# Placing the operands of a matmul-bound hybrid block at a fixed distance in SBUF

## The chip, the cores and the metric

One NeuronCore of a Trainium2 chip runs the whole block. The metric is device time in microseconds of one execution, the median of several runs. Beside it there is one profiled execution of the same program, whose trace the views below read.

## The reference

One residual layer with two branches over 16 meta tokens and 512 tokens, model width 2048, all in float32:

```python
h = rms_norm(x, norm_g)
proj = h @ w_in                      # 2048 x 12368
(q_a, k_a, v_a, z_a, q_i, k_i, w_i, q_b, f_b, i_b, z_b, gates) = jnp.split(proj, cuts, axis=-1)
...
# branch A: per query a ReLU indexer scores the keys, the top 128 are kept, attention over them
o_a = dsa_attention(q, k, v, qi, ki, wi, chunk_ids, topk)
y_a = o_a.reshape(B, T, BRANCH_WIDTH) * jax.nn.silu(z_a)
# branch B: gated linear recurrence S_t = diag(f_t) S_{t-1} + k_t v_t^T, chunkwise
o_b = rms_norm(hgrn2_chunkwise(qb, 1.0 - f, vb, jnp.log(f)), hgrn_out_norm_g)
y_b = o_b.reshape(B, T, BRANCH_WIDTH) * jax.nn.silu(z_b)
p = jnp.einsum('btnc,ncd->btnd', jnp.stack([y_a, y_b], axis=2), w_branch)
merged = jnp.sum(jax.nn.sigmoid(gates.reshape(B, T, N_BRANCH, D)) * p, axis=2)
return x + merged @ w_out
```

## The kernel before, in words

Every large product is made of three matmuls in the type float32r: an operand is split into a high part (the value rounded to float32r) and a low part (the rest), and high x high, high x low and low x high are summed in PSUM. ScalarE makes the high part of a weight, VectorE (or a DMA that adds) the low part; both are in the helper `hi_lo`, into the tiles `wh` and `wl`, which rotate over three buffers each.

The kernel walks through a list of jobs. The first are ordinary ("in"): the indexer's key and queries and two gates of branch B, with moving operands of 512 columns. Then come 43 pairs ("pair"): each takes two blocks of 128 columns of `w_in` and uses a Strassen-like scheme, in which seven products of half size take the place of eight. Tokens are split in two halves of 264 (8 meta tokens and 256 others), the 2048 rows of the weights in two halves of 1024. The seven products have names:

```python
SEVEN = (("11", "11", "x", 0), ("s2", "t2", "y", 0), ("12", "21", "x", 1), ("s3", "t3", "y", 1),
         ("s1", "t1", "z", 0), ("22", "t4", "w", 0), ("s4", "22", "z", 1))
```

The first column names the weight operand (a raw block or a sum of blocks), the second the token operand, the third the PSUM bank. Each product is 8 steps k of three matmuls, 24 in all, 168 in a pair. In pairs the weights are stationary and the tokens move, with 256 columns, or 264 where the meta tokens are wanted (`w=264`: key/value pairs and forget/input pairs). The token operands lie in `hH`, `hL` (16 tiles each, the two halves side by side, 1056 bytes apart) and in `tT` (the sums t1 and t2 in tiles `a` and `b`, t4 with its high part in the first half of a tile and its low part in the second). They are made once and stay to the end of the pairs.

After the pairs come 32 branch jobs ("br", 24 matmuls of 512 columns each; weights stationary, `yH` and `yL` moving), among which the attention of the eight heads is run, and at the end 8 output jobs ("out"), the same scheme as the pairs with the tokens (`mh`) stationary and the weights moving, 256 columns.

All temporaries and the long-lived token operands live in 70 equal slots of 528 float32 a partition, 2112 bytes, handed out by the class `Slots`. The program's order is written out by a planner: each engine has a clock, each instruction a cost, and a slot remembers when its last user ends by these clocks. `Slots.get` took the free slot that had been free longest. Work beside the matmuls (top-k, normalisation and rotation of queries and keys, the recurrence, the attention) is in tasks with priorities, which `pump` advances between the matmuls as long as the clocks of VectorE and ScalarE are not too far ahead of TensorE's. Each engine then runs its own instructions in that order. Weights arrive by SP's queue, sums of weight blocks are made by VectorE and by adding DMAs on POOL's queue, and a pair's results go to DRAM over SP's queue.

Beside the slots there are fixed tiles: `tabQ` and `tabK` (rotary tables multiplied by the norms' gains, made in `consts`), `MT`, and `bias0` to `bias3` for the top-k mask. `consts` was started at the eighth job, among the indexer's queries. Gate pairs (16 of them) are spread over the list by `gate_pair`.

A matmul's two operands are read at addresses in SBUF that follow from slot and weight tile. The slots begin 2112 bytes apart, which is 64 more than a multiple of 256. The weight tiles were 4096 bytes long and began at multiples of 256, and their parts are 512 or 1024 bytes long.

Of the kernel before, what the change touches and what calls it, by code (L numbers as in the profile page):

```python
# [38 lines left out]
SAME = {"pe": 0.0, "act": 60.0, "dve": 125.0, "pool": 60.0}  # L39
MARGIN = 300.0  # L40
NSLOT = 70
NZ = 2
# [103 lines left out]
class Slots:  # L146
    def __init__(self, core, pool, tags, shape, space):
        self.core, self.pool, self.shape = core, pool, shape
        self.free = list(tags)
        self.last = {t: (0.0, "pe") for t in tags}  # L150
        self.tag = {}
        self.k = 0
        self.peak = 0
        self.total = len(tags)

    def get(self, name, dt=F32):
        assert self.free, "out of " + name
        t = min(self.free, key=lambda x: self.last[x][0])
        self.free.remove(t)
        self.peak = max(self.peak, self.total - len(self.free))  # L160
        self.k += 1
        a = self.pool.tile(self.shape, dt, name=f"{name}_{self.k}", tag=t)
        nm = a.tensor.name
        self.tag[nm] = t
        self.core.ac[nm] = self.last[t]
        return a
# [17 lines left out]
def hybrid_kernel(ctx, tc, x, meta, vecs, w_in, rows, w_branch, w_out,  # L184
# [8 lines left out]
    E = Core(nc)  # L193
    S = Slots(E, sp, [f"s{i}" for i in range(NSLOT)], [128, T], None)
    B1 = Slots(E, pp, [f"b{i}" for i in range(6)], [128, 512], None)
    B2 = Slots(E, pp, ["c0"], [128, 2, 512], None)
# [67 lines left out]

    def slots(name, n=1, dt=F32):
        return [S.get(name, dt) for _ in range(n)]

    def slot(name, dt=F32):
        return S.get(name, dt)

# [20 lines left out]
    for c in range(2):  # L291
        s = wp.tile([128, 1024], F32, name=f"xm{c}", tag=f"wh{c}")
# [3 lines left out]
    tabs = slots("tabs", 2)  # L296
    tabA = tabs[0][:, 0:320].rearrange("p (b d) -> p b d", b=5)
    RB = tabs[0][:, 320:512]
    tabI = tabs[1][:, 0:160].rearrange("p (b d) -> p b d", b=5)
    wi = tabs[1][:, 160:224].rearrange("p (b d) -> p b d", b=4)  # L300
    masks = cp.tile([128, 256], U8, name="masks")
# [85 lines left out]

    def hi_lo(k, src, m):
        h = wp.tile([128, 1024], F32R, name=f"wh{k}", tag=f"wh{k % NWS}")
        l = wp.tile([128, 1024], F32R, name=f"wl{k}", tag=f"wl{k % NWS}")  # L390
        E.act(h[:, :m], src, AF.Copy)
        if 8 <= k < 22:
            n = l[:, :m]
            E.act(n, h[:, :m].bitcast(F32), AF.Copy, scale=-1.0)
            E.dma_add(n, src.bitcast(F32R))
        else:
            (E.ptt if k < 6 else E.tt)(l[:, :m], src, h[:, :m].bitcast(F32), OP.subtract)
        return h, l

    def split_chunk(k, ch):  # L400
        load_upto(ch["i"])
        m = ch["nk"] * ch["ncols"]
        r, nk, n = ch["raw"], ch["nk"], ch["ncols"]
        ch["h"], ch["l"] = [], []
        if k < 4:
            for g in range(2):
                h, l = slot("eh", F32R), slot("el", F32R)
                w = 4 * n
                E.act(h[:, :w], r[:, w * g:w * g + w], AF.Copy)
                (E.ptt if k > 1 else E.tt)(l[:, :w], r[:, w * g:w * g + w], h[:, :w].bitcast(F32), OP.subtract)  # L410
                early.extend((h, l))
                ch["h"] += [h[:, n * i:n * i + n] for i in range(4)]
                ch["l"] += [l[:, n * i:n * i + n] for i in range(4)]
        else:
            h, l = hi_lo(k, r[:, :m], m)
            ch["h"] = [h[:, n * i:n * i + n] for i in range(nk)]
            ch["l"] = [l[:, n * i:n * i + n] for i in range(nk)]
        load_upto(ch["i"] + NRAW)
# [22 lines left out]
    def prep_op(k, op):  # L441
# [20 lines left out]
    cvec = cp.tile([128, 35], F32, name="cvec")  # L462
    MT = cp.tile([128, 256], F32, name="MT")
    lbt = fp.tile([128, 8, 4], F32, name="lbt")
    gq1 = fp.tile([128, 2], F32, name="gq1")
    tabQ = cp.tile([128, 4, 64], F32, name="tabQ")
    tabK = cp.tile([128, 5, 64], F32, name="tabK")

    def consts():
# [11 lines left out]
        E.dve([gq1], [], 2, lambda v: v.memset(gq1[0:32, :], 1.0))  # L481
        for t, o, nb in ((tabQ, 64, 4), (tabK, 128, 5)):
# [86 lines left out]
    kk = []  # L569
    CQ, SQ = slot("cq"), slot("sq")  # L570

# [56 lines left out]
    def idx_task(j, xq):  # L628
# [53 lines left out]
        if not idx_left[0]:  # L682
            S.put(kkH, kkL, CQ, SQ, tabs[1])
            for qt in range(4):
                topk_tasks.append(spawn(topk_task(qt), 6))
# [6 lines left out]
    first_two = []  # L692
    bias = [cp.tile([128, k], BF16, name=f"bias{k}") for k in KQ]

# [89 lines left out]
    def tokens(src, x, d, tab, name):  # L784
# [23 lines left out]
        E.tt(yv, yv, r[:, None, 8:12, None].to_broadcast([128, 4, 4, 32]), OP.mult)  # L808
        yield E.clk["pe"]
        v = y[:, 0:128].rearrange("p (c d) -> p c d", c=4)  # L810
        a = sq[:, 0:128].rearrange("p (c d) -> p c d", c=4)
# [9 lines left out]
    def ka_task(g, xk):  # L821
        y = yield from tokens({(0, 256): xk[:, 8:264], (2, 256): xk[:, 272:528]}, xk, kd_[g][:, 16:528],
                              tabK[:, 0:4, :], "ka")
        yield from room(1)
# [3 lines left out]
        spawn(fan_out(kd_[g][:, 16:528], tb, e, ("k", g)), 0)  # L828
        if g == 3:
# [5 lines left out]
            y, e = yield from norm_rope(pb[:16].rearrange("p (b d) -> p b d", b=4), 16, 4,  # L835
                                        tabK[:16, 4:5, :].to_broadcast([16, 4, 64]), "km")
            B1.put(pb)
            yield e
            yield E.clk["pe"] + 3000.0
# [58 lines left out]
    def q_task(h, xq):  # L898
        y = yield from tokens({(0, 512): xq[:, :512]}, xq, qd_[h], tabQ, "qa")
# [4 lines left out]
        spawn(fan_out(qd_[h], tb, e, ("q", h)), 0)  # L904

    att, raws, got = {}, {}, set()
# [13 lines left out]
    def att_task(h):  # L920
# [22 lines left out]
        for qt in (3, 2, 1, 0):  # L943
# [6 lines left out]
            else:  # L950
                if qt:
                    pb = yield from bank("plg")
                vs[qt] = pb[:, :kq] if qt else pb[:, KQ[1]:KQ[1] + kq]
# [46 lines left out]
    def pv_task(h, ps, e):  # L1000
# [69 lines left out]
        yield e  # L1070
        yH[0, h], yL[0, h] = slot("yH", F32R), slot("yL", F32R)
        E.act(yH[0, h][:, :512], z[:, :512], AF.Copy)
# [18 lines left out]
    def hgrn_task(h, prev):  # L1091
# [6 lines left out]
        while not LB:  # L1098
            yield WAIT
        while ready() < 5:  # L1100
            yield WAIT
# [298 lines left out]
    def tops_task(i):  # L1400
# [3 lines left out]
        for k in range(4 * i, 4 * i + 4):  # L1404
# [320 lines left out]
    jobs[3].pre = pre_t  # L1725
    jobs[7].pre = lambda: spawn(consts(), 2)
    jobs[-1].pre = lambda: (sum_1(jobs[ji]), sum_2(jobs[ji]), hold.append(1))
# [16 lines left out]
    for h in range(0, 8, 2):  # L1744
        two(A[h], A[h + 1])
    for g in range(4):
# [4 lines left out]
        if g in (1,):  # L1751
            gate_pair()
    for h in range(8):
# [3 lines left out]
        if h == 0:  # L1757
            jobs[-1].pre = lambda: E.more.update(act=130.0, dve=85.0)
        for _ in range((1, 2, 1, 2, 1, 2, 1, 2)[h]):
            gate_pair()  # L1760
# [216 lines left out]
```

## Time and profile before

| | |
|---|---|
| median of 3 runs | 1481.22 us (1479.68 to 1481.84) |
| profiled execution | 1480.5 us, its span 1478.7 us |
| granted TensorE clock | 1.000 |
| TensorE busy | 1465.2 us, 12544 matmuls |
| VectorE busy | 1187.8 us |
| ScalarE busy | 712.6 us |
| GpSimd busy | 271.9 us |
| moved by DMA | 263.25 MB |

The span is the time from the first to the last instruction. Matmuls overlap in flight: one is recorded for about 0.28 us and the next starts well before it ends, so busy time says little about TensorE, and the distance from one start to the next is what is to be read. PE are the matmuls, PEld the loads of the stationary operand, DVE is VectorE, ACT ScalarE, POOL GpSimd. Addresses of operands are not in the profile; they are those of the compiled program.

### The profile page before, as it was taken

To read this page: it belongs to the slowest core of one execution; us is meant where nothing else is said; L and a number is where in the kernel's file an instruction comes from. 1 tells how busy PE (TensorE), PEld (TensorE's weight loads), DVE (VectorE), ACT (ScalarE), POOL (GpSimd) and SP (SyncE) were. 2 spreads that over 40 slices of the span, in tenths; PEclk is the share of its full clock that TensorE was granted. 3 is DMA by queue.
4 is the path that set the end of the run, shared out by engine and by line. 5 is a ranking of instruction groups with operands and counts; after the bars stand their busy time and mean duration, and the time that the engine had idled before them with its cause. 6 is when DMAs were issued, how large, how long until landed. Compare 5 with 4: busy or idle time off the path is not lost.

```text
span 1478.7 us, 31334 instructions
## 1 busy us (share of the span) xinstructions
PE 1465.2 (99%) x12544; PEld 1396.4 (94%) x12544; DVE 1187.8 (80%) x2017; ACT 712.6 (48%) x1170; POOL 271.9 (18%) x346
## 2 busy tenths in 40 slices
PE   7999999999999999999999999999999999999999
PEld 6888899999999999999999999999998888889998
DVE  6698899999998888788887887888676755878776
ACT  5576644444444454444444444444467752334332
POOL 2211000003313320101001011000367110103221
PEclk9999999999999999999999999999999999999999
DMA  9266577877888977767787686857896335448873
GB/s 275 76 158 152 143 172 186 188 182 193 214 210 218 240 173 183 179 168 182 172 194 165 171 193 158 200 144 191 198 286 167 111 109 155 147 131 221 213 212 90
DMA packets 336066, 263.25 MB, mean 178 GB/s; under 512 B 32484, under 2 KB 303408, under 8 KB 335920
## 3 DMA queue, kind: packets, MB, share of 16 engines
q1 hardware_dynamic: 306160, 174.51, 41.2%
q0 software_dynamic: 24256, 80.45, 28.1%
q10 hardware_dynamic: 5504, 6.29, 1.3%
q8 instruction: 98, 1.61, 0.4%
q14 instruction: 48, 0.39, 0.1%
HBM read 170.40 MB, written 29.98 MB: 136 GB/s over the span
## 4 chain that ended last, share of the span: by engine, by line
PE 97%; DVE 2%; ACT 0%; DMA 0%; issue 0%; POOL 0%; DVEq 0%; POOLq 0%
PE pg L93 20%; PE px L91 17%; PE pz L91 16%; PE py L91 16%; PE po L91 11%; PE pw L91 8%; PE psc L93 1%; PE phl L93 1%; PE pov L91 1%; PE plg L93 1%; PE pho L93 1%; PE ppt L97 1%; PE px L97 1%; PE phs L93 0%; DMA vrow<-in_vecs_dram 0%; PE pw L97 0%
## 5 line engine op out<-in xcount | busy, mean ns | idle before, releaser
L101 ACT ACTIVATE wh<-raw 128x1024 fp32r<-128x1024 f32 x305 | 323.4, 1061 | 483.5 <-PE pz L91 130.8
L108 DVE TENSOR_TENSOR wl<-raw,wh 128x1024 fp32r<-128x1024 f32 x289 | 356.6, 1234 | 100.5 <-ACT wh L101 99.5
L91 PE MATMUL px<-hH,wh 128*128 128x256 f32 (+1 forms) x688 | 195.6, 284 | 0.0
L91 PE MATMUL px<-hH,wl 128*128 128x256 f32 (+1 forms) x688 | 194.1, 282 | 0.0
L91 PE MATMUL px<-hL,wh 128*128 128x256 f32 (+1 forms) x688 | 193.6, 281 | 0.0
L101 ACT ACTIVATE wh<-sum 128x1024 fp32r<-128x1024 f32 x102 | 108.2, 1060 | 156.0 <-PE py L91 41.9
L91 PE MATMUL po<-wh,mh 128*128 128x256 f32 x896 | 158.0, 280 | 0.0
L108 DVE TENSOR_TENSOR wl<-sum,wh 128x1024 fp32r<-128x1024 f32 x102 | 131.0, 1284 | 29.2 <-ACT wh L101 28.6
L91 PEld LDWEIGHTS po<-wh,mh 128*128 128x128 f32 x896 | 137.1, 188 | 0.0
L91 PEld LDWEIGHTS px<-hH,wh 128*128 128x128 f32 x688 | 129.4, 188 | 0.5
L91 PEld LDWEIGHTS px<-hH,wl 128*128 128x128 f32 x688 | 129.5, 188 | 0.0
L91 PEld LDWEIGHTS px<-hL,wh 128*128 128x128 f32 x688 | 129.4, 188 | 0.0
L91 PE MATMUL pz<-tT,wh 128*128 128x256 f32 (+1 forms) x688 | 127.1, 284 | 0.0
L91 PE MATMUL pw<-tT,wh 128*128 128x256 f32 (+1 forms) x688 | 126.4, 284 | 0.0
L91 PE MATMUL po<-wl,mh 128*128 128x256 f32 x448 | 125.3, 280 | 0.0
L91 PE MATMUL py<-tT,wh 128*128 128x256 f32 (+1 forms) x688 | 125.2, 282 | 0.0
L117 POOL DMA_DIRECT2D raw<-raw x51 | 44.2, 868 | 363.2 <-DVE sum L108 340.6
L91 PEld LDWEIGHTS pz<-tT,wh 128*128 128x128 f32 x688 | 105.7, 188 | 0.2
L91 PEld LDWEIGHTS pw<-tT,wh 128*128 128x128 f32 x688 | 105.6, 189 | 0.2
L91 PEld LDWEIGHTS py<-tT,wh 128*128 128x128 f32 x688 | 105.7, 188 | 0.0
L93 PE MATMUL pg<-yH,wh 128*128 128x512 f32 x256 | 103.3, 403 | 0.0
L93 PE MATMUL pg<-yH,wl 128*128 128x512 f32 x256 | 101.0, 394 | 0.0
(319 smaller groups left out, 3870.8 us busy)
## 6 DMA issues: line engine op xcount, KB each, us to landing
raw<-in_w_in_dram SPq DMA_DIRECT2D x192, 512.0 KB, 4.6
raw<-raw POOLq DMA_DIRECT2D x51, 512.0 KB, 5.4
raw<-sum POOLq DMA_DIRECT2D x51, 512.0 KB, 5.4
raw<-in_w_branch_dram SPq DMA_DIRECT2D x32, 512.0 KB, 4.8
raw<-in_w_out_dram SPq DMA_DIRECT2D x32, 512.0 KB, 4.1
gd<-g SPq DMA_DIRECT2D x32, 256.0 KB, 4.5
g<-gd POOLq DMA_DIRECT2D x30, 256.0 KB, 3.3
wl<-raw POOLq DMA_DIRECT2D x14, 512.0 KB, 4.6
```

The costliest lines, as they stand in the source:

```text
L91: self.nc.tensor.matmul(out, lhsT, rhs, start=start, stop=stop, skip_group_check=True)
L93: self.nc.tensor.matmul(out, lhsT, rhs, start=start, stop=stop)
L97: self.nc.tensor.transpose(out, in_, ident)
L101: self.nc.scalar.activation(out, in_, f, **kw)
L108: self.nc.vector.tensor_tensor(out, a, b, op=op)
L117: self.nc.gpsimd.dma_start(out, a, accum_op=OP.add)
```

## The change

It leaves the arithmetic as it is and moves operands. `Slots.get` takes a wanted residue, a "home": a slot's number mod 4, which decides its address mod 256. It prefers a free slot of that home, unless that would have to be waited for 1.5 us longer by the planner's clocks; without a home, it takes a slot that need not be waited for, those of residue 3 first, then 2, 1 and 0. The kinds of token operands get homes (`HOME`, `YHOME`). Weight tiles become 1088 elements long, and `hi_lo` puts the parts at an offset, which `lead` works out from the home of the operand that they will meet.

```diff
+DIST = 192
+DPO = 192
+DBR = 192
+HOME = {"11": (0, 0), "s2": (2, 1), "12": (1, 0), "s3": (0, 1), "s1": (2, 0), "22": (3, 0), "s4": (1, 1)}
+YHOME = (3, 0)
...
-    def get(self, name, dt=F32):
+        self.order = [3, 2, 1, 0]
+
+    def get(self, name, dt=F32, home=None):
         assert self.free, "out of " + name
-        t = min(self.free, key=lambda x: self.last[x][0])
+        now = self.core.clk["pe"]
+        res = lambda x: int(x[1:]) % 4
+
+        def key(x):
+            wait = max(self.last[x][0] - now, 0.0)
+            if home is None:
+                return (wait, self.order.index(res(x)), self.last[x][0])
+            return (wait + (0.0 if res(x) == home else 1500.0), self.last[x][0])
+
+        t = min(self.free, key=key)
...
+    for i in range(NSLOT):
+        sp.tile([128, T], F32, name=f"home{i}", tag=f"s{i}")
...
+    def lead(home, byte, turn=False):
+        return (64 * home + byte + (DPO if turn else -DIST)) % 256 // 4
...
-    def hi_lo(k, src, m):
-        h = wp.tile([128, 1024], F32R, name=f"wh{k}", tag=f"wh{k % NWS}")
-        l = wp.tile([128, 1024], F32R, name=f"wl{k}", tag=f"wl{k % NWS}")
+    def hi_lo(k, src, m, o):
+        h, l = (wp.tile([128, 1088], F32R, name=f"w{i}{k}", tag=f"w{i}{k % NWS}")[:, o:o + 1024] for i in "hl")
...
-            h, l = hi_lo(k, r[:, :m], m)
+            j = ch["job"]
+            o = lead(YHOME[j.n], DIST - DBR) if j.kind == "br" else lead(ch["k0"] // 8, 32)
+            h, l = hi_lo(k, r[:, :m], m, o)
...
-        h, l = hi_lo(k, src, 1024)
+        home, half = HOME[nm]
+        h, l = hi_lo(k, src, 1024, lead(home, 0, True) if pr.kind == "out" else
+                     lead(home, 1056 * half + 4 * (264 - pr.w)))
...
-            hH.append(slot("hH", F32R))
-            hL.append(slot("hL", F32R))
+            hH.append(slot("hH", F32R, kt // 8))
+            hL.append(slot("hL", F32R, kt // 8))
...
-            a, b, t4 = slots("tT", 3, F32R)
+            a, b, t4 = slots("tT", 2, F32R, 2) + [slot("tT", F32R, 3)]
...
-            yH[n, h], yL[n, h] = slot("yH", F32R), slot("yL", F32R)
+            yH[n, h], yL[n, h] = slots("yH", 2, F32R, YHOME[n])
...
-            h, l = o[nm] = slots("mh", 2, F32R)
+            h, l = o[nm] = slots("mh", 2, F32R, "abc".index(nm))
...
-        h = o["d"] = slot("mh", F32R)
+        h = o["d"] = slot("mh", F32R, 3)
```

Around it, tiles and order move a little. `tabQ` and `tabK` become two slots that are returned after the twelve key and query tasks; the indexer's table goes into `MT`; the cosines `CQ` share one fixed tile with the four `bias` parts, which are set up when the indexer is done (`first_bias`). `consts` starts with the sixth pair, the third of the four z_a pairs, instead of the eighth job. One gate pair moves from behind the second forget/input pair to the key/value stage (`if g in (1,)` becomes `if g in (0, 3)`, and the first `2` in `(1, 2, 1, 2, 1, 2, 1, 2)[h]` becomes `1`). A head of the recurrence starts with four ready slots instead of five, and the attention's first three banks must be ready as well as returned (`bank("plg", True)`).

More of the change, by code (lines that the diff above doesn't have):

```diff
@@ L263, in ready, with slots, slot @@
         return sum(S.last[t][0] <= E.clk["pe"] for t in S.free)
[L265 to L269, printed above, removed]
+    def slots(name, n=1, dt=F32, home=None):
+        return [S.get(name, dt, home) for _ in range(n)]
+    def slot(name, dt=F32, home=None):
+        return S.get(name, dt, home)
+    def lead(home, byte, turn=False):
+        return (64 * home + byte + (DPO if turn else -DIST)) % 256 // 4
     X = {}
@@ L291, in hybrid_kernel @@
     for c in range(2):
-        s = wp.tile([128, 1024], F32, name=f"xm{c}", tag=f"wh{c}")
+        s = wp.tile([128, 1088], F32, name=f"xm{c}", tag=f"wh{c}")[:, :1024]
         nc.sync.dma_start(s[:NM, :], meta[:, 1024 * c:1024 * c + 1024])
@@ L295, in hybrid_kernel @@
     load_x(1, nc.sync)
-    tabs = slots("tabs", 2)
+    MT = cp.tile([128, 256], F32, name="MT")
+    tabs = slots("tabs", 1)
     tabA = tabs[0][:, 0:320].rearrange("p (b d) -> p b d", b=5)
     RB = tabs[0][:, 320:512]
-    tabI = tabs[1][:, 0:160].rearrange("p (b d) -> p b d", b=5)
-    wi = tabs[1][:, 160:224].rearrange("p (b d) -> p b d", b=4)
+    tabI = MT[:, 0:160].rearrange("p (b d) -> p b d", b=5)
+    wi = MT[:, 160:224].rearrange("p (b d) -> p b d", b=4)
     masks = cp.tile([128, 256], U8, name="masks")
@@ L462, in hybrid_kernel, with turn_done @@
     cvec = cp.tile([128, 35], F32, name="cvec")
-    MT = cp.tile([128, 256], F32, name="MT")
     lbt = fp.tile([128, 8, 4], F32, name="lbt")
     gq1 = fp.tile([128, 2], F32, name="gq1")
-    tabQ = cp.tile([128, 4, 64], F32, name="tabQ")
-    tabK = cp.tile([128, 5, 64], F32, name="tabK")
+    turns, turned = {}, [12]
+    def turn_done():
+        turned[0] -= 1
+        if not turned[0]:
+            S.put(*turns["slots"])
     def consts():
@@ L481, in consts @@
         E.dve([gq1], [], 2, lambda v: v.memset(gq1[0:32, :], 1.0))
-        for t, o, nb in ((tabQ, 64, 4), (tabK, 128, 5)):
+        turns["slots"] = slots("turns", 2)
+        for n, o, nb, t in (("q", 64, 4, turns["slots"][0]), ("k", 128, 5, turns["slots"][1])):
+            t = turns[n] = t[:, :64 * nb].rearrange("p (b d) -> p b d", b=nb)
             E.tt(t[:, :, 0:32], tabA[:, :nb, 0:32], RB[:, None, o:o + 32].to_broadcast([128, nb, 32]), OP.mult)
@@ L569, in hybrid_kernel @@
     kk = []
-    CQ, SQ = slot("cq"), slot("sq")
+    CQ, SQ = cp.tile([128, 672], F32, name="CQ", tag="bias"), slot("sq")
     def ki_task(kw):
@@ L682, in idx_task @@
         if not idx_left[0]:
-            S.put(kkH, kkL, CQ, SQ, tabs[1])
+            S.put(kkH, kkL, SQ)
+            first_bias()
             for qt in range(4):
@@ L692, in hybrid_kernel, with first_bias @@
     first_two = []
-    bias = [cp.tile([128, k], BF16, name=f"bias{k}") for k in KQ]
+    bias = []
+    def first_bias():
+        t = cp.tile([128, 1344], BF16, name="bias", tag="bias")
+        E.ac[t.tensor.name] = E.ac[CQ.tensor.name]
+        for k in KQ:
+            o = sum(b.shape[1] for b in bias)
+            bias.append(t[:, o:o + k])
     def topk_task(qt):
@@ L809, in tokens @@
         yield E.clk["pe"]
+        tab = turns[tab][:, 0:4, :]
         v = y[:, 0:128].rearrange("p (c d) -> p c d", c=4)
@@ L822, in ka_task @@
         y = yield from tokens({(0, 256): xk[:, 8:264], (2, 256): xk[:, 272:528]}, xk, kd_[g][:, 16:528],
-                              tabK[:, 0:4, :], "ka")
+                              "k", "ka")
         yield from room(1)
@@ L828, in ka_task @@
         spawn(fan_out(kd_[g][:, 16:528], tb, e, ("k", g)), 0)
-        if g == 3:
+        if g < 3:
+            turn_done()
+        else:
             yield from room(3)
@@ L835, in ka_task @@
             y, e = yield from norm_rope(pb[:16].rearrange("p (b d) -> p b d", b=4), 16, 4,
-                                        tabK[:16, 4:5, :].to_broadcast([16, 4, 64]), "km")
+                                        turns["k"][:16, 4:5, :].to_broadcast([16, 4, 64]), "km")
             B1.put(pb)
+            turn_done()
             yield e
@@ L898, in q_task @@
     def q_task(h, xq):
-        y = yield from tokens({(0, 512): xq[:, :512]}, xq, qd_[h], tabQ, "qa")
+        y = yield from tokens({(0, 512): xq[:, :512]}, xq, qd_[h], "q", "qa")
         yield from room(1)
@@ L904, in q_task @@
         spawn(fan_out(qd_[h], tb, e, ("q", h)), 0)
+        turn_done()
     att, raws, got = {}, {}, set()
@@ L951, in att_task @@
                 if qt:
-                    pb = yield from bank("plg")
+                    pb = yield from bank("plg", True)
                 vs[qt] = pb[:, :kq] if qt else pb[:, KQ[1]:KQ[1] + kq]
@@ L1070, in pv_task @@
         yield e
-        yH[0, h], yL[0, h] = slot("yH", F32R), slot("yL", F32R)
+        yH[0, h], yL[0, h] = slots("yH", 2, F32R, YHOME[0])
         E.act(yH[0, h][:, :512], z[:, :512], AF.Copy)
@@ L1099, in hgrn_task @@
             yield WAIT
-        while ready() < 5:
+        while ready() < 4:
             yield WAIT
@@ L1725, in hybrid_kernel @@
     jobs[3].pre = pre_t
-    jobs[7].pre = lambda: spawn(consts(), 2)
     jobs[-1].pre = lambda: (sum_1(jobs[ji]), sum_2(jobs[ji]), hold.append(1))
@@ L1745, in hybrid_kernel @@
         two(A[h], A[h + 1])
+        if h == 4:
+            jobs[-1].pre = lambda: spawn(consts(), 2)
     for g in range(4):
@@ L1750, in hybrid_kernel @@
         two(QA[2 * g], QA[2 * g + 1])
-        if g in (1,):
+        if g in (0, 3):
             gate_pair()
@@ L1758, in hybrid_kernel @@
             jobs[-1].pre = lambda: E.more.update(act=130.0, dve=85.0)
-        for _ in range((1, 2, 1, 2, 1, 2, 1, 2)[h]):
+        for _ in range((1,1,1,2,1,2,1,2)[h]):
             gate_pair()
```

## The prediction

> **What bounds the kernel now.** I read the page first, then the waits of TensorE, then windows that lie inside one kind of matmul, then the order in time of single matmuls.
>
> ```profile
> span 1478.7 us, 31334 instructions
> PE 1465.2 (99%) x12544; PEld 1396.4 (94%) x12544; DVE 1187.8 (80%) x2017; ACT 712.6 (48%) x1170; POOL 271.9 (18%) x346
> PE 97%; DVE 2%; ACT 0%; DMA 0%; issue 0%; POOL 0%; DVEq 0%; POOLq 0%
> ```
>
> TensorE is 97% of the chain that ended last. The waits of TensorE by what released it say the same: after the first load nothing of weight is left to remove.
>
> ```profile
> PE pc L97 <- DMA vrow<-in_vecs_dram: 8.5, 1, 8.5
> PE pz L91 <- DVE g L108: 1.1, 3, 0.7
> PE px L97 <- DVE x L122: 0.3, 1, 0.3
> ```
>
> So the number of matmuls is fixed and the time between the starts of two of them is the whole question. Windows inside one kind of work give it (columns: window and length, busy time with instructions of PE, PEld, DVE, ACT, POOL, granted clock, DMA share, GB/s; first pairs of width 256, then a pair of width 264, then the branch matmuls of 512 columns, then the output matmuls; the last two are DVE-heavy stages).
>
> ```profile
> 185.00:310.00 125.00, 125.00 (x1060) 125.00 (x1059) 119.36 (x230) 56.17 (x68) 11.06 (x13) 1.00 0.77 182
> 314.50:333.50 19.00, 19.00 (x158) 19.00 (x157) 17.95 (x29) 8.59 (x11) 1.70 (x2) 1.00 0.75 175
> 1225.00:1290.00 65.00, 65.00 (x282) 52.58 (x281) 43.34 (x69) 19.73 (x28) 7.47 (x14) 1.00 0.48 143
> 1320.00:1430.00 110.00, 110.00 (x939) 110.00 (x938) 84.47 (x84) 46.58 (x50) 29.64 (x22) 1.00 0.82 222
> 185.00:333.00 148.00, 148.00 (x1250) 148.00 (x1249) 141.02 (x264) 66.26 (x80) 12.76 (x15) 1.00 0.78 182
> 370.00:444.00 74.00, 74.00 (x622) 74.00 (x622) 69.36 (x124) 35.89 (x79) 17.97 (x24) 1.00 0.86 212
> ```
>
> A window also counts the two or so matmuls that reach over its edge (each is in flight about 0.28 us, 0.40 for 512 columns). Without them the time per matmul is 125/(1060-2.4) = 118.2 ns, 19/(158-2.4) = 122.1, 65/(282-1.7) = 231.9 and 110/(939-2.4) = 117.4. The clock is 1.00 throughout, so none of this is the throttle.
>
> Is there anything below 118? The rows of single matmuls in the output stage, in order of time, answer it (start, time in flight, instruction, how many merged):
>
> ```profile
> 1343.75 0.28 PE L91 MATMUL po<-wl,mh 128*128 128x256 f32 x1
> ...
> 1344.77 0.28 PE L91 MATMUL po<-wl,mh 128*128 128x256 f32 x1
> ...
> 1345.47 0.28 PE L91 MATMUL po<-wl,mh 128*128 128x256 f32 x1
> ...
> 1346.19 0.28 PE L91 MATMUL po<-wl,mh 128*128 128x256 f32 x1
> ...
> 1346.66 0.40 PE L91 MATMUL po<-wh,mh 128*128 128x256 f32 x2
> ...
> 1347.37 0.40 PE L91 MATMUL po<-wh,mh 128*128 128x256 f32 x2
> ```
>
> From 1343.75 to 1344.77 there are nine matmuls: 113.3 ns each. From 1345.47 to 1346.19 six of the same shape: 120. The operands' places tell them apart. A slot is 528 x 4 = 2112 bytes, that is 64 mod 256, so slots fall on four residues; a weight tile and its parts of 512 or 1024 bytes are all 0 mod 256. Call d the moving operand's address less the stationary one's, mod 256, from the addresses in the compiled program, taken in program order beside the trace. In the first stretch d is 192 for eight of the nine; in the second it is 0, 128, 0, 0, 128, 64. In the third, from 1346.66 to 1347.37, five of six have d = 192 and the pace is 118. So 192 does not act at once. The output stage has 25 stretches of six to twelve matmuls with d = 192; one in the first of them and one in the last are these rows, both at three matmuls in 0.34 us:
>
> ```profile
> 1332.47 0.28 PE L91 MATMUL po<-wl,mh 128*128 128x256 f32 x1
> 1332.81 0.28 PE L91 MATMUL po<-wl,mh 128*128 128x256 f32 x1
> ...
> 1474.08 0.28 PE L91 MATMUL po<-wl,mh 128*128 128x256 f32 x1
> 1474.42 0.28 PE L91 MATMUL po<-wl,mh 128*128 128x256 f32 x1
> ```
>
> 21 of the 25 fall to 113 or 114 after one to four matmuls; 4, among them the third stretch above, stay at 118. None that had reached 113 left it before d changed. Without the first two and the last step of each, all 25 average 113.8.
>
> **The change part by part.** It touches no matmul count: 43 input pairs of 168 matmuls (12 of width 264, the key/value and the forget/input pairs, 2016 in all, and 31 of width 256, 5208), 8 x 168 = 1344 in the output stage, 1200 of 512 columns.
>
> *Distance, 256-wide pairs.* Slots get homes by residue, and the weight parts start at an offset that makes d = 192; one role (the fourth transformed operand, op 22) has its low part half a slot on, at d = 192 + 32 = 224, for a third of its 24 matmuls. Ends: 113.3 (all settle) and 118.3 (the third stretch). I take 113.9, by the 25 stretches, since here d stays put for hundreds of matmuls. 4464 x (118.2 - 113.9) = 19.2 us. The other 744 I give half: 744 x 2.1 = 1.6.
>
> *Output stage.* There the weights move, and the offset has the other sign: 1344 x (117.4 - 113.9) = 4.7 us.
>
> *Width 264.* A stretch of four with d = 192 is all that the trace has:
>
> ```profile
> 327.08 0.40 PE L91 MATMUL pz<-tT,wh 128*128 128x264 f32 x2
> 327.32 0.28 PE L91 MATMUL pz<-tT,wl 128*128 128x264 f32 x1
> 327.44 0.41 PE L91 MATMUL pz<-tT,wh 128*128 128x264 f32 x2
> ```
>
> Three matmuls in 0.36 us, 120. Ends: no gain, 122.1; and the settled pace plus what eight more columns cost, 113.3 + 122.1 - 118.2 = 117.2. I take 120.1, the row itself: 2016 x 2.0 = 4.0 us.
>
> *512 columns.* The longest such stretch outside the attention is three:
>
> ```profile
> 1225.19 0.40 PE L93 MATMUL pg<-yH,wh 128*128 128x512 f32 x1
> 1225.42 0.40 PE L93 MATMUL pg<-yL,wh 128*128 128x512 f32 x1
> 1225.66 0.39 PE L93 MATMUL pg<-yH,wl 128*128 128x512 f32 x1
> 1225.89 0.39 PE L93 MATMUL pg<-yH,wh 128*128 128x512 f32 x1
> ```
>
> 0.70 us for three, 233.3 against 231.9. Ends: 1.4 x 1200 = 1.7 us lost, and a gain of 4.9 per instruction as in the settled 256, 5.9 us. I take 0, between, as the only stretch points the wrong way.
>
> *Writes at an offset.* ACT and DVE write the same 1024 elements, and the tiles are only longer in memory: nothing added. No row has such a write at an offset; if it cost DVE 1%, that is 3.6 us of 1187.8, covered except in the DVE-heavy stages.
>
> *Choice of slots.* Before, the slot that had been free longest was taken; now a free slot of the last residue, and up to 1.5 us of planned waiting is accepted for a home. In the pairs 56 of 70 slots are held for good, so about nine are rotated instead of 14. What is queued behind a late slot is ACT's or DVE's next write, and behind that the weight parts. The cover is that ACT waits for TensorE, not the other way:
>
> ```profile
> ACT wh L101 <- PE pz L91: 130.8, 80, 3.0
> ACT wh L101 <- PE py L91: 84.8, 69, 2.4
> ACT wh L101 <- PE px L91: 83.4, 50, 3.0
> ACT wh L101 <- DVE sum L108: 39.7, 14, 8.3
> ```
>
> 299 us of such waits in all over 199 occasions, 1.5 each. A slot that is up to 1.5 us late costs nothing; beyond that each late slot costs TensorE the rest.
>
> *Tables and gates.* The rotary tables go from fixed tiles into two slots, other tables and the index cosines into fixed tiles: no instruction added. Their making moves from the index stage to the sixth of the paired gate stages, inside 185 to 333: four products and some ten tiny operations, estimated at 3 us of DVE from the rows of the rotary products, 0.24 and 0.29 us each. One gate pair moves from the recurrence to the key/value stage, 168 matmuls, with its four weight loads, two adds on POOL's queue and two stores on SP's. The stage it enters has 0.86 DMA share, which a pair without token transfers thins; the recurrence still ends with five gate pairs after its last head, about 100 us. Costs nothing. Attention waits for a bank that is free, not just returned: order only, branch matmuls fill.
>
> ```profile
> L108 DVE TENSOR_TENSOR qas<-qay,tabQ 128x64 f32<-128x64 f32 (+1 forms) x18 | 3.4, 242 | 0.2
> L108 DVE TENSOR_TENSOR qay<-qas 128x128 f32<-128x128 f32 x6 | 1.8, 292 | 0.2
> ```
>
> *What is late next.* DVE. In 185 to 333 it is free for 148 - 141.0 = 7.0 us, in 370 to 444 for 4.6. A pace of 113.9 takes 3.6% off these 222 us, 8.1, and the tables take 3: 11.1 of 11.6. The top-k steps among DVE's work can slip, so it fits, barely; between nothing and the whole 8.1 I charge 3 us for it and the slots.
>
> **Sum.** -19.2 - 1.6 - 4.7 - 4.0 + 0 + 3 = -26.5 us. The profiled execution took 1480.5 us, 1478.7 of span and 1.8 around it: 1454.0. The median of the runs is 0.7 higher: 1455.
>
> **The rivals.**
>
> *DVE becomes the bound* in the stages above: none of the 8 us there come, TensorE waits for weight parts: 1455 + 9 = 1464. For it, 95% busy; against it, top-k.
>
> *Everything settles.* 4464 x 4.9 + 744 x 2.4 + 1344 x 4.1 + 2016 x 4.9 + 1200 x 4.9 = 45 us, less the charge of 3: 1439.
>
> *The distance is not the cause*, the stretches at 113.3 owe it to something else of the output stage: 1481. Against it, same shape, same stage, and d = 0 next to it at 120. The Trainium skill speaks for it: "TensorE: Matmul & The Clock Gate", in its step-by-step section, says that TensorE has two independent read ports and that loading the next weights takes nothing from the running matmul, and "SBUF — State Buffer", on the two sides, says that TensorE's port waits on nobody. By that rule no address can matter and the sum would be the charge alone. The rows at 113.3 and 120 disagree with it.
>
> *Slower: the long uniform stretch falls into the slow rhythm*, as at 1346.66. Then 256-wide pairs stay (118.3), the output stage loses 0.9 x 1344 = 1.2 us, the 512-column matmuls 1.7, and the charge of 3 stays: 1481.2 + 5.9 = 1487. It decides from where the slow share s makes 113.3(1 - s) + 118.3 s exceed 118.2, s = 0.98; in the trace it is 4 of 25, but once in, no stretch was long enough to see it end.
>
> **How the numbers follow.** Forecast 0.55, DVE 0.17, everything 0.12, not the cause 0.07, slow rhythm 0.09. A measurement here tells 0.2%, 3 us. The first three are faster: 0.84. "Not the cause" is 0.06 the same and 0.01 slower; with the slow rhythm 0.10 slower. The range holds the first three: from a little below 1439 to above 1464, where half of the gain is lost, 1436 to 1473; it leaves out 0.16.
>
> **What would show it.** In the windows of one kind: some 1097 matmuls in 125 us of 256-wide pairs (114.2 each, the 744 included) instead of 1060, some 968 in 110 us of the output stage instead of 939. In single rows, long series at 113 or 114. If the pace is 118, the cause or the rhythm was wrong; if it is 114 in the output stage and TensorE waits for DVE's weight parts between 185 and 444, DVE took it. 512-column windows should keep 232. I would be wrong most easily on widths 264 and 512, where the trace has almost no uniform stretch.

## The result and the profile after

| | before | after |
|---|---|---|
| median | 1480.49 us (1479.68 to 1481.84) | 1466.99 us (1466.14 to 1468.26) |
| span of the profiled execution | 1478.7 us | 1464.4 us |
| time after over time before | | 0.9909, interval 0.9891 to 0.9926 |

The kernel became faster by 13.5 us. The forecast was 26 us, so the direction was right and the size was half.

The head of the page of the changed kernel, with the shares of its chain:

```profile
span 1464.4 us, 31517 instructions
PE 1448.0 (99%) x12544; PEld 1378.0 (94%) x12544; DVE 1183.1 (81%) x2017; ACT 715.7 (49%) x1172; POOL 272.5 (19%) x346
PE 93%; DVE 3%; DMA 2%; issue 1%; ACT 1%; POOL 0%; SPq 0%; DVEq 0%; POOLq 0%; ACTq 0%
```

TensorE still sets the time, though its share of the chain fell from 97% to 93%: as many matmuls, 17 us less of them in flight. Its waits (us in total, times, longest):

```profile
PE pc L102 <- DMA vrow<-in_vecs_dram: 7.9, 1, 7.9
PE pw L96 <- DVE attn L1209: 1.5, 3, 0.5
PE pz L96 <- DVE g L113: 0.9, 2, 0.5
PE pg L98 <- DVE pTL L113: 0.9, 1, 0.9
```

No row names a weight part. The saving therefore has to be read from the pace, in the windows that the prediction used:

```profile
185.00:310.00 125.00, 125.00 (x1087) 125.00 (x1086) 121.40 (x239) 59.97 (x72) 11.03 (x13) 1.00 0.80 187
314.50:333.50 19.00, 19.00 (x162) 19.00 (x161) 17.91 (x29) 7.48 (x10) 1.34 (x2) 1.00 0.79 188
1320.00:1430.00 110.00, 110.00 (x948) 110.00 (x947) 81.39 (x79) 45.58 (x48) 31.96 (x23) 1.00 0.82 218
185.00:333.00 148.00, 148.00 (x1278) 148.00 (x1277) 143.35 (x276) 70.15 (x85) 12.73 (x15) 1.00 0.80 188
370.00:444.00 74.00, 73.45 (x622) 73.27 (x621) 70.48 (x128) 34.02 (x65) 18.91 (x28) 1.00 0.85 210
```

With 2.4 taken off for the edges, as before: 256-wide pairs 125/1084.6 = 115.2 ns (it was 118.2, forecast 114.2), the 264-wide pair 119.0 (122.1), the output stage 110/945.6 = 116.3 (117.4, forecast 113.9). The same can be done over all matmuls: for each, the time from its start to the next one's, in program order, with the addresses of the compiled program beside it. Below, "pace" is the mean of these over one kind of matmul, without starts that come 25 ns or more after the kind's median; the time lost in those is the "late starts".

| kind | matmuls | pace before | pace after | pace x count | late starts before, after |
|---|---|---|---|---|---|
| pairs, 256 wide | 5208 | 118.25 ns | 115.30 ns | -15.4 us | 8.0, 9.2 us |
| pairs, 264 wide | 2016 | 121.79 | 121.13 | -1.3 | 3.4, 4.8 |
| output stage | 1344 | 117.41 | 116.37 | -1.4 | 0.0, 0.0 |
| branch jobs, 512 columns | 768 | 231.87 | 231.54 | -0.3 | 2.5, 4.3 |
| indexer and gates, 512 columns | 432 | 233.22 | 233.03 | -0.1 | 0.3, 0.3 |

The paces give -18.5 us, the late starts +4.4; the first wait for a load was 0.6 shorter in this execution. That is -14.7, where the spans differ by 14.3.

In the 256-wide pairs the distances are as intended: 4898 of the 5208 matmuls have 192, 248 have 224 (the low part in product 22), and 62, in s2 and s1, have 64 because a slot missed its home. In the branch jobs only 384 of 768 have 192. Yet the 256-wide matmuls at 192 don't share one pace. By product, before and after:

| product | 11 | s2 | 12 | s3 | s1 | 22 | s4 |
|---|---|---|---|---|---|---|---|
| before, ns | 118.19 | 117.60 | 118.31 | 118.18 | 118.21 | 118.50 | 118.75 |
| after, ns | 114.78 | 114.13 | 114.77 | 116.82 | 113.94 | 118.78 | 113.87 |

Product 22 gained nothing; s3 gained a third of what the others did. One pair of the changed kernel in order of time shows it (start, time in flight; one row for each step k: 12 in `px`, then s3 in `py`):

```profile
257.84 0.28 PE L96 MATMUL px<-hL,wh 128*128 128x256 f32 x1
...
259.88 0.28 PE L96 MATMUL px<-hL,wh 128*128 128x256 f32 x1
260.23 0.28 PE L96 MATMUL py<-hL,wh 128*128 128x256 f32 x1
...
261.99 0.28 PE L96 MATMUL py<-hL,wh 128*128 128x256 f32 x1
```

Product 12 runs through six steps of three matmuls in 2.04 us, 113.3 ns each; s3, right behind it, through five in 1.76 us, 117.3 each. Nothing waits and d is 192 in both. So there are two rhythms at one distance, and within a product the rhythm mostly holds. What differs is the step from one product to the next: the address of the last moving operand less that of the next stationary one, mod 256. It is 32 or 96 ahead of 11, s2, 12, s1 and s4, 128 ahead of 22 and 224 ahead of s3.

### The profile page after: what moved, and what is told of

Read it like the earlier page. It is cut to its first block, busy times and chain, and to the rows that moved or that the text cites. A ratio compares the mean times of both kernels' runs of the same rounds, so it can differ in the third digit from the quotient of the medians.

```text
span 1464.4 us, 31517 instructions
## 1 busy us (share of the span) xinstructions
PE 1448.0 (99%) x12544; PEld 1378.0 (94%) x12544; DVE 1183.1 (81%) x2017; ACT 715.7 (49%) x1172; POOL 272.5 (19%) x346
## 4 chain that ended last, share of the span: by engine, by line
PE 93%; DVE 3%; DMA 2%; issue 1%; ACT 1%; POOL 0%; SPq 0%; DVEq 0%; POOLq 0%; ACTq 0%
PE pg L98 20%; PE px L96 16%; PE pz L96 15%; PE py L96 15%; PE po L96 11%; PE pw L96 8%; PE psc L98 1%; PE phl L98 1%; PE pov L96 1%; PE plg L98 1%; PE pho L98 1%; DVE wl L113 1%; PE ppt L102 1%; DMA raw<-raw 1%; PE px L102 1%
## 5 line engine op out<-in xcount | busy, mean ns | idle before, releaser
L98 PE MATMUL pg<-yH,wh 128*128 128x512 f32 x512 | 162.9, 399 | 1.0 <-DVE pTL L113 0.9
L96 PE MATMUL pz<-tT,wh 128*128 128x256 f32 (+1 forms) x688 | 122.9, 280 | 0.0
L98 PEld LDWEIGHTS pg<-yH,wh 128*128 128x128 f32 x512 | 93.2, 188 | 21.3 <-PE pg L98 1.3
```

The source lines that it names most:

```text
L96: self.nc.tensor.matmul(out, lhsT, rhs, start=start, stop=stop, skip_group_check=True)
L98: self.nc.tensor.matmul(out, lhsT, rhs, start=start, stop=stop)
```

## The experiments

Theory A: the pace follows the distance d, and among matmuls with d = 192 the step between two products picks the rhythm. The rivals are that the moved work or the order of instructions made the gain, and that the slow products wait for something else.

### The distance taken out

All else as in the changed kernel, so the same slots, homes and order:

```diff
-DIST = 192
-DPO = 192
-DBR = 192
+DIST = 0
+DPO = 0
+DBR = 0
```

> Homes, slots, tables and order as in the changed kernel; only the weight parts' offset differs, so that the distance is 0 instead of 192 (32 where it was 224). If the distance is the cause, 256-wide pairs go from 115.3 ns to about 119.7, the pace that the output stage had at distance 0, and the output stage from 116.4 to 119.5: 5208 x 4.4 + 1344 x 3.1 = 27 us more, about 1494, slower than the kernel before. If it is the choice of slots or the moved work, the time stays near 1467.

1487.72 us, ratio to before 1.0052 (1.0037 to 1.0067): slower than before, and 20.7 us slower than the changed kernel. The window of 256-wide pairs, and that of the output stage:

```profile
185.00:310.00 125.00, 125.00 (x1051) 125.00 (x1050) 118.33 (x233) 58.38 (x71) 11.05 (x13) 1.00 0.77 183
1320.00:1430.00 110.00, 110.00 (x910) 109.41 (x909) 79.72 (x83) 46.10 (x50) 26.30 (x21) 1.00 0.79 211
```

1051 matmuls where d = 192 has 1087, and 910 for 948. The paces are 119.18 (256-wide), 119.37 (output), 120.80 (264-wide), and the 512-column ones are faster than with 192: 230.75 and 230.51. The distance makes the difference: one uniform distance is bad and another good. The steps changed with it, but they do not explain the loss: they are 96 ahead of 11, s2, 12 and s4 and 32 ahead of s3, the values that stand ahead of the fast products of the changed kernel, and these five run at 119.2 to 119.8 here.

### The moved work alone

The old choice of slots and no offset; tables, gate pair and thresholds as in the changed kernel:

```diff
-        t = min(self.free, key=key)
+        t = min(self.free, key=lambda x: self.last[x][0])
...
     def hi_lo(k, src, m, o):
+        o = 0
```

> Tables, gate pair and the moved work as in the changed kernel, but slots chosen as before (free longest) and no offset in the weight tiles, so the distances are mixed again. If the distance is the cause, 256-wide pairs are back at 118.2 and the time at 1480 to 1483. If the moved work brought the gain, 1467.

1483.07 us, 1.0019 (1.0009 to 1.0029): what was moved costs 2.7 us. The paces are those of before (118.27, 121.83, 117.69), and late starts in the pairs grow from 11.4 to 14.5 us. The window of 256-wide pairs, and a wait of this kernel that the profile before does not have:

```profile
185.00:310.00 125.00, 125.00 (x1059) 125.00 (x1059) 119.26 (x234) 58.85 (x71) 11.04 (x13) 1.00 0.77 184
PE py L96 <- DVE p L113: 1.9, 2, 1.6
```

So the choice of slots and the offsets together brought about 16 us (1483.1 to 1467.0), and the moved work took 2.7 of what they would have brought to the kernel before.

### Other steps between the products, same distance

The two halves of `hH` trade homes. The step becomes 96 ahead of s3 (224 before), 160 ahead of 11 and s1 (32 and 96 before), and 96 ahead of s2, 12 and s4 (32 before):

```diff
-HOME = {"11": (0, 0), "s2": (2, 1), "12": (1, 0), "s3": (0, 1), "s1": (2, 0), "22": (3, 0), "s4": (1, 1)}
+HOME = {"11": (1, 0), "s2": (2, 1), "12": (0, 0), "s3": (1, 1), "s1": (2, 0), "22": (3, 0), "s4": (0, 1)}
...
```

(The output stage keeps its homes, the branch operands take the second half of theirs, and the order in which slots without a home are taken changes with the trade.)

> The homes of the two halves of the normalised tokens are exchanged (weight offsets follow, output stage unchanged), so distance 192 stays, but the step from one product to the next changes: last moving operand less next stationary one was 224 before s3 and is 96, and is 96, 128 or 160 before the others. Theory A, the step decides which of the two rhythms a product falls into (after 32 and 96 nearly all ran at 113 to 114, after 224 most at 118): s3 falls from 116.8 to about 114, 2 us less, 1465, if 160 is no worse. Theory B, the slow rhythm belongs to the operand of s3 itself: s3 stays at 117, 1467.

1468.63 us, 0.9921 (0.9906 to 0.9936). On the whole nothing changed, and within it three products did: s3 went from 116.82 to 114.02, 11 from 114.78 to 116.46 and s1 from 113.94 to 117.52. The same pair as above, now with 11 and s3:

```profile
252.39 0.28 PE L97 MATMUL px<-hL,wh 128*128 128x256 f32 x1
...
254.87 0.28 PE L97 MATMUL px<-hL,wh 128*128 128x256 f32 x1
...
260.69 0.28 PE L97 MATMUL py<-hL,wh 128*128 128x256 f32 x1
...
261.71 0.28 PE L97 MATMUL py<-hL,wh 128*128 128x256 f32 x1
```

Seven steps of 11 in 2.48 us are 118.1 ns for a matmul, three of s3 in 1.02 us are 113.3. A step of 160 took a fast series into the slow rhythm in 40 of 42 cases (a product counts as fast or slow by its mean pace). That s3 was slow for its place in the pair, or for want of a weight part, is out.

### All distances

Each job gets its own distance, 0, 32, ... 224 in turn (the index and gate jobs, the pairs by width, the branch jobs and the output jobs each counted for themselves):

```diff
+    def dist_of(j):
+        if j.kind == "br":
+            return 32 * (j.c0 // 128 % 8)
+        same = [i for i in jobs if i.kind == j.kind and getattr(i, "w", 0) == getattr(j, "w", 0)]
+        return 32 * (same.index(j) % 8)
...
```

> Homes as in the changed kernel, but the distance is another one in each pair, branch, index and output job: 0, 32, 64, ... 224 in turn. It measures the pace of every width at every distance in one run. If the distance is the cause, 256-wide pairs at 192 run at 113 to 115 and those at 0 at 119 to 120 in the same run; the whole is near the kernel before, 1478 to 1485. If 192 only works when everything else stands at 192 too, its pairs stay at 118. For widths 264 and 512 I expect no distance more than 2 ns better than 192.

One run, 1483.67 us. Pace in ns, by the distance at which each matmul stands (256-wide without product 22). It rests on few jobs: three or four 256-wide pairs for each distance, one or two 264-wide pairs and one output job:

| d | 0 | 32 | 64 | 96 | 128 | 160 | 192 | 224 |
|---|---|---|---|---|---|---|---|---|
| 256-wide pairs | 119.4 | 117.2 | 117.3 | 119.7 | 118.7 | 118.1 | 114.8 | 118.3 |
| output stage | 119.5 | 117.1 | 117.7 | 119.6 | 119.0 | 117.8 | 116.7 | 118.2 |
| 264-wide pairs | 121.0 | 121.8 | 121.0 | 123.5 | 120.7 | 122.0 | 121.2 | 120.4 |
| branch, 512 | 229.8 | 232.8 | 230.6 | 233.8 | 231.9 | 233.3 | 233.1 | 232.4 |

192 is the best distance for 256 columns and for no other width. For 264 columns it lies in the middle, and 512 columns are fastest at 0. Product 22 lies between 117.6 and 118.9 at every distance; a third of its matmuls stand 32 off whatever one sets.

### The steps in the output stage

Homes and starting columns of the `mh` operands are chosen so that the steps become 32, 96 and 192 in place of 0, 64 and 128:

```diff
+OPLACE = {"a": (0, 8), "b": (2, 16), "c": (3, 0), "d": (1, 8)}
...
-            h, l = o[nm] = slots("mh", 2, F32R, "abc".index(nm))
+            oh, oc = OPLACE[nm]
+            h, l = o[nm] = [q[:, oc:oc + 512] for q in slots("mh", 2, F32R, oh)]
```

> Output stage only: the token tiles of the four kinds get other homes, and three kinds start 8 or 16 columns into their slot, so that the step from one product to the next (last moving less next stationary) is 32, 96 or 192 instead of 0, 64 or 128. Distance stays 192. Theory A (the step sets the rhythm; 32 and 96 lead to the fast one, an unbroken 192 keeps it): output stage from 116.4 to 113.5 to 114.3, 3 to 4 us less than the changed kernel, 1463. Theory B (the slow rhythm of the output stage belongs to its operands or comes by chance): 116 to 117 and 1467.

1466.95 us, 0.9909 (0.9894 to 0.9924): no different from the changed kernel. The pace did fall, from 116.37 to 115.06, 1.8 us over the stage, and not to the 113.5 to 114.3 of theory A. The addresses tell them apart: of the stage's 56 products only 32 have all 24 matmuls at 192. Of these 32, 31 are fast, at 114.1 on the average; the other 24, which hold two or four matmuls whose operand missed its home, average 116.4. Products 12 and s4 are of both sorts, at the same step: 113.4 in the four jobs without a miss, about 117 in the four with one. So theory A holds where the distance does, but for one product, and that has two late starts in it. The stage also has 2.6 us of late starts where it had none, and the profile names them:

```profile
PE po L98 <- DVE wl L115: 1.7, 3, 0.9
```

```profile
1320.00:1430.00 110.00, 108.34 (x936) 107.71 (x935) 82.60 (x78) 45.34 (x49) 29.92 (x23) 1.00 0.81 215
```

TensorE is idle for 1.66 of the 110 us here, the waits being for low parts of weights: a faster series ran into its own supply. Outside the output stage no run has such a row for a low part.

### Product 22 with one distance

In the 256-wide pairs the low part of t4 is replaced by its high part, so that all matmuls of product 22 have d = 192; the contribution of the low part is left out, and that of the high part enters twice:

```diff
+                if tn == "t4" and w == 256:
+                    tl = th
```

> In pairs of width 256, product 22 reads the high part of its token operand where the low part belongs, so the low part's contribution is left out of the result; the count of matmuls is the same and all stand at 192 instead of a third at 224. If the mixed distance makes product 22 slow (118.8 in the changed kernel), it falls to 113.5 to 115 and the whole by 744 x 4.5 = 3.3 us, 1463. If the product itself is slow (its step in is 128), it stays at 118 to 119 and 1467.

1466.25 us, 0.9905 (0.9891 to 0.9920). Product 22 goes from 118.78 to 117.22, 1.2 us over its 744 matmuls: with one distance it runs in the slow rhythm, and no longer at a pace above it. Its step is 128, and behind a fast s1 it fell into the slow rhythm in 25 of 26 cases.

### The other widths

Distance 0 for the 512-column jobs (by the addresses it holds for all index and gate matmuls and for 384 of the 768 of the branch jobs), 224 for the 264-wide pairs:

```diff
-DBR = 192
+DBR = 0
...
-            o = lead(YHOME[j.n], DIST - DBR) if j.kind == "br" else lead(ch["k0"] // 8, 32)
+            o = lead(YHOME[j.n], DIST - DBR) if j.kind == "br" else lead(ch["k0"] // 8, 32 + DIST)
...
-                     lead(home, 1056 * half + 4 * (264 - pr.w)))
+                     lead(home, 1056 * half + 4 * (264 - pr.w) - (32 if pr.w == 264 else 0)))
```

> Only the distance of the other widths is changed: index and branch jobs (512 columns) to 0, pairs of width 264 to 224. From the sweep's rows: 432 x 2.5 for the index jobs, 768 x 0.8 for the branch jobs, 2016 x 0.8 for width 264, 3.3 us in all, 1463 to 1464. If those paces were an accident of the sweep, 1467.

1465.96 us, 0.9903 (0.9888 to 0.9918). The 512-column matmuls gained, in the direction that the table by distance has: 233.03 to 230.47 in the index and gate jobs (1.1 us), 231.54 to 230.73 in the branch jobs (0.6 us). The 264-wide ones gained 1.1 us (121.13 to 120.59). Against that stand product 11 of the 256-wide pairs, which went from 114.78 to 115.62 without any distance of its own changed, and 1.9 us more of late starts in the 256-wide pairs. All of 11's loss lies in the 12 pairs that follow a 264-wide one: 11 is in the slow rhythm there in 11 of them, where the changed kernel has 4. The step ahead of 11 is 0 there in both kernels, so what differs is the series before it. The whole is within the error of the changed kernel.

### Part of the order put back

The tables at the old place, five ready slots again for a head of the recurrence, and the attention's banks as before; the gate pair stays moved:

```diff
-                    pb = yield from bank("plg", True)
+                    pb = yield from bank("plg")
...
-        while ready() < 4:
+        while ready() < 5:
...
+    jobs[7].pre = lambda: spawn(consts(), 2)
...
-        if h == 4:
-            jobs[-1].pre = lambda: spawn(consts(), 2)
```

> Distances as in the changed kernel; the making of the tables goes back to the index stage, a head of the recurrence waits for five ready slots again and the attention's banks need not be ready. The kernel with the moved work and without the distances took 2.7 us more than the kernel before. If these three parts are that cost: 1464 to 1465. If it is the gate pair, which stays moved, or the tiles: 1467.

1473.26 us, 0.9951 (0.9935 to 0.9968): 6.3 us slower than the changed kernel, and so not a way to get back the 2.7 us of the moved work. By the addresses, slots missed their homes: 186 of the 256-wide matmuls now have d = 64 or 128 (62 in the changed kernel), all in s2 and s1, whose paces went from 114.13 and 113.94 to 115.55 and 115.09. The kind as a whole went from 115.30 to 115.78, 2.5 us, with 1.8 more of late starts; the 264-wide pairs lost 1.0 in pace. In the attention two waits appear that the changed kernel does not have:

```profile
PE plg L98 <- DVE pTL L113: 1.6, 1, 1.6
PE pg L98 <- ACT wh L106: 1.3, 1, 1.3
```

So part of the moved order is what lets the slots find their homes. Which of the three edits it is stays open.

### Bad steps on purpose

The distance stays, at 4960 matmuls of 5208. Only homes and halves move: `hH`'s second half goes to the third home and t1, t2 to the second, and t1 and t2 trade sides in their tiles.

```diff
-HOME = {"11": (0, 0), "s2": (2, 1), "12": (1, 0), "s3": (0, 1), "s1": (2, 0), "22": (3, 0), "s4": (1, 1)}
+HOME = {"11": (0, 0), "s2": (1, 0), "12": (2, 0), "s3": (0, 1), "s1": (1, 1), "22": (3, 0), "s4": (2, 1)}
...
-                     "t1": (a[:, lo], b[:, lo]), "t2": (a[:, hi], b[:, hi]), "t4": (t4[:, lo], t4[:, hi]),
+                     "t1": (a[:, hi], b[:, hi]), "t2": (a[:, lo], b[:, lo]), "t4": (t4[:, lo], t4[:, hi]),
...
```

> Every 256-wide pair matmul keeps the distance 192 (4960 of 5208 at 192, even 62 more than in the changed kernel); only the places among themselves are others: the second operand's half goes to the third home, the summed operands to the second, and their two halves trade sides. By the compiled program the step between two products (last moving address less next stationary address, mod 256) becomes 128 ahead of s2, 12 and s1, 224 ahead of s4, 32 ahead of s3, 96 ahead of 22 and of the next pair's 11. Theory A (the step between products picks one of two rhythms, 32 and 96 the fast one near 114 ns, 128 and 224 the slow one near 117.7): s2, 12, s1 and s4 go from about 114.2 to 117.7 (4 x 744 x 3.5 = 10.4 us more), s3 from 116.8 to about 114 (2.1 us less); the whole near 1475, 8 us above the changed kernel, at an unchanged distance. Theory B (the distance alone sets the pace, the slow products are slow for another reason, such as their weight parts being late): all products stay where they are and the time is 1466 to 1468.

1472.12 us, 0.9941 (0.9929 to 0.9954). The time rose by 5.1 us, 4.1 of them in the pace of the 256-wide pairs, whose distance is unchanged. So theory B is out, but theory A had named 8. By product: 11 113.61, s2 117.76, 12 114.78, s3 114.54, s1 117.41, 22 118.67, s4 115.89. The products s2, s1 and s3 did as forecast. 12 did not: its step is 128 too, and it is fast. One pair:

```profile
255.16 0.28 PE L97 MATMUL py<-tT,wl 128*128 128x256 f32 x1
...
257.64 0.28 PE L97 MATMUL py<-tT,wl 128*128 128x256 f32 x1
...
258.23 0.28 PE L97 MATMUL px<-hL,wh 128*128 128x256 f32 x1
...
260.26 0.28 PE L97 MATMUL px<-hL,wh 128*128 128x256 f32 x1
```

s2 has 118.1 ns (seven steps in 2.48 us), 12 behind it 112.8 (six in 2.03). A step of 128 does not set the slow rhythm, it changes the rhythm: into s2 from fast to slow in 28 of 28 cases, into s1 in 24 of 25, into 12 from slow to fast in 24 of 30, and in 15 of 15 where no other matmul stands inside or between the two products. With that, 12's 2.6 us of the 10.4 don't come; s4, half slow and half fast, gives 1.5 in place of 2.6.

### What the runs point to

The output stage's steps of the one run and the distance 0 for 512 columns of the other, without the change to the 264-wide pairs:

```diff
-DBR = 192
+DBR = 0
+OPLACE = {"a": (0, 8), "b": (2, 16), "c": (3, 0), "d": (1, 8)}
...
-            o = lead(YHOME[j.n], DIST - DBR) if j.kind == "br" else lead(ch["k0"] // 8, 32)
+            o = lead(YHOME[j.n], DIST - DBR) if j.kind == "br" else lead(ch["k0"] // 8, 32 + DIST)
...
```

> The version that the runs point to: the output stage's operands moved so that the steps between its products are 32, 96 or 192, and in the 512-wide jobs distance 0 in place of 192. By the rows of the runs before, the 512-wide index jobs should take 230.5 ns in place of 233.0 (432 x 2.5 = 1.1 us less), the branch jobs about 230.7 in place of 231.5 (0.6 us less), the output stage 115.1 in place of 116.4 (1.7 us less), of which waits for weight parts took back 2.6 us. Theory A (these gains are what the paces say): 1464.5 to 1466, no more than 2 us under the changed kernel, a difference that the runs can hardly tell. Theory B (the waits that the faster output stage opens take everything back): 1467 or above.

1465.12 us, 0.9899 (0.9883 to 0.9914), against 0.9909 (0.9891 to 0.9926) for the changed kernel: the lowest median of all, not told apart from it. Its profiled span is 2.9 us shorter, 1461.5. The paces add: 230.50 and 230.70 for 512 columns, 115.02 in the output stage, where again 32 of 56 products have all matmuls at 192: these 32 are all fast, and none of the other 24 is. The stage's wait is shorter this time (0.3 us in one wait, 0.6 us of late starts), so that it held what the faster pace gave:

```profile
PE po L98 <- DVE wl L115: 0.3, 1, 0.3
```

```profile
1320.00:1430.00 110.00, 109.70 (x955) 109.49 (x954) 80.96 (x79) 45.72 (x49) 31.89 (x23) 1.00 0.81 221
```

955 matmuls, where the changed kernel has 948.

## Why the prediction was right or wrong

**The cause** was right: with the distance taken out and every instruction in its place, the gain is gone and more (1487.7). The rival "the distance is not the cause" fell with it. The Trainium skill ("TensorE: Matmul & The Clock Gate", the step-by-step section) says that loading the next weights takes no SBUF read bandwidth from the running matmul. The prediction concluded from it that no address could matter, and that conclusion does not hold here: with nothing but the weight parts' addresses changed, the pace of the 256-wide pairs went from 119.2 to 115.3. Whether two reads meet at all, no trace here shows.

**256-wide pairs**, the term that failed most in us. The 4464 matmuls outside product 22 were put at 113.9 ns, 19.2 us; they measured 114.7, 15.6 us less than before. The step of the argument that was wrong is "21 of the 25 fall to 113": it took settling as a matter of a few matmuls at a constant d. In the changed kernel a series is broken every 24 matmuls, and the step at the break sets the rhythm anew; 224 ahead of s3 turns the fast one, in which 12 mostly ends, into the slow one. The third stretch of the prediction, at 118, was this rhythm, and it was priced as a rare case.

**Product 22** was given half of the gain, 1.6 us. It got none (118.50 to 118.78). The third of its matmuls off the distance is only a part of that: with all of them at 192 it still took 117.2, since the step of 128 behind a fast s1 puts it into the slow rhythm.

**Output stage**: 4.7 us forecast, 1.4 measured, for the same reason and worse. With steps of 0, 64 and 128 five of seven products lie between 116.1 and 117.9, and one at 114.06. Moving the steps brought 115.0, and 113.9 to 114.1 in the products whose operands all found their homes.

**Width 264**: 4.0 forecast, 1.3 measured. Both ends of the 2.0 ns were read from one place. The 122.1 came from one window of one pair; over all twelve the pace before was 121.8. The 120 came from three matmuls; it is indeed the median at d = 192, but these series also hold single starts of 122 to 132, and their mean is 121.1. By the table of distances, no other distance would have brought as much as 1 ns.

**512 columns** kept their 232, as forecast: 0.4 us of gain in all. The branch jobs test this only by half, since 384 of their 768 matmuls are not at 192.

**The charge of 3 us**: the late starts took 4.4. The moved work was said to cost nothing but 3 us of DVE; by itself it cost 2.7 us (1483.1 to 1480.3 before). The cause was not DVE as the bound. The rival "DVE becomes the bound" said that TensorE would wait for weight parts, and no such row came, though DVE's free time between 185 and 333 fell from 7.0 to 4.6 us. ScalarE went on waiting for TensorE, so that cover held:

```profile
ACT wh L106 <- PE pz L96: 116.5, 71, 2.9
ACT wh L106 <- PE px L96: 80.6, 46, 2.7
ACT wh L106 <- PE py L96: 80.4, 73, 2.4
```

277.5 us, in place of 299. That the time came out near this rival's 1464 is chance: the gain was missing in the pace, not in waits. The slow part of the range, up to 1473, was there for this rival, so the range holds the measured time for another reason than the one it was drawn for.

**The slow rhythm** as a rival supposed that the whole would fall into it. It is real and took its share of products, s3 and much of the output stage, but it ends at the next break.

Of the 12.2 us missing in the span (26.5 - 14.3), 3.6 are the pairs' six products, 1.6 product 22, 3.3 the output stage, 2.7 the width 264 and 1.4 the late starts; 0.4 came from 512 columns. These sum to 12.2; the 0.6 us of the shorter first wait, on the other side, is about the error of such a sum.

## What to carry over

Where a kernel is bound by streams of small matmuls and its pace lies above the best that its trace shows anywhere, sort the single starts by the operands' addresses: here 4 ns of 119 hung on the distance between moving and stationary operand mod 256 (119.2 at 0, 115.3 at 192). Measure the pace for each width, since the best distance of one (192 at 256 columns) was not that of another (0 at 512). And don't price a short stretch's pace over a whole kernel without asking what breaks a long series: here the step at each break decided which of two rhythms followed. Read from the compiled program whether the operands lie where they were meant to: single misses cost whole products.

## What the runs showed that was not expected

- At d = 192 and 256 columns there are two stable rhythms, about 113.3 and 117.7 ns for a matmul, with no wait between them. Which one holds is set where one product follows another. A step of 32 or 96 led to the fast one, from either rhythm, in nearly all cases; 160 and 224 led from the fast to the slow one (40 of 42; 22 of 25 in the changed kernel), 224 from slow to fast in 4 of 4; 0, 64 and 128 mostly changed the rhythm. Most exceptions come from counting whole products. Counted right at the break, with no other matmul, no start of 140 ns or more and no matmul off the distance within six matmuls ahead of it and nine behind, the pairs of the changed kernel and of the seven runs that keep its distance in them follow one table: 32 or 96 led to the fast rhythm in 578 of 579 cases, 160 from fast to slow in 37 of 37, 224 changed the rhythm in 120 of 120 and 128 in 77 of 82. (Most of these runs share their layout, so the cases repeat.) In the output stage 128 behind a slow product stayed slow in all 19, so this is a description, not a mechanism.
- Since the operands' places differ by multiples of 32 and both good steps are odd multiples of it, seven products in a ring can't all be entered by one: the seven steps add up to the seven distances, and 7 x 192 is an even multiple of 32. That is worked out from the addresses, and no run goes beyond the homes shown.
- Product series of mixed distance (192 and 224, two to one) run at 118.8, no faster than with places at random (118.5).
- 264 columns have no distance with a pace below 120.4 in the table, eight columns above 256 at 114.8. Why is open; so is what in the hardware the 256 bytes belong to, and whether it is a matmul's own stationary operand or the next one's that counts: inside a product both lie at the same place mod 256.
